# Weight halves 64 bytes into wider tiles, in a decoder trunk on one core

## The chip, the core and the metric

One of the eight cores of a Trainium2 chip runs the kernel. The metric is the device time of one execution in microseconds, taken as the median of several runs. A profile of one further execution of the kernel before is at hand, with its own time.

## The reference

The reference is a decoder trunk of two layers on 256 positions of width 2048, all in float32. Cut to what matters here:

```python
for layer in range(DEPTH):                                # 2
    shift, scale, gate = _adaln(c, ada_w[layer], ada_b[layer])
    h = x * (1.0 + scale) + shift
    if layer < N_A_LAYERS:                                # layer 0
        y = _ssd_mixer(h, a_in_w[i], ..., a_out_w[i])     # 2048 -> 10304, conv, scan, gate, 4096 -> 2048
    else:                                                 # layer 1
        y = _dilated_mixer(h, k_sh, v_sh, b_in_w[i], b_out_w[i])
    x = _layer_norm(ALPHA * x + (1.0 + gate) * y, ln_g[layer], ln_b[layer])
    if layer == N_A_LAYERS - 1:
        k_sh, v_sh = _shared_kv(x, kv_w)                  # 2048 -> 6144
```

Inside the mixer of layer 0, each of 8 groups forms scores from its B and C heads, masks them causally, and weights them by decays:

```python
cb = jnp.einsum("blgn,bsgn->blsg", cc, bc)
y_diag = jnp.einsum("blsgk,bsgkp->blgkp", cb[..., None] * decay, xc)
```

Most of the arithmetic lies in the big products of activations and weights (in_w, out_w, kv_w and the like).

## The kernel before

Weights stream in as pieces of 128 partitions by 1024 columns of float32 (`load_piece`, the tile `raw`, six buffers). `split` makes two halves of each piece in a rounded float32 type (`fp32r`): ScalarE copies the piece to `whi` (line 99), VectorE subtracts to get the remainder `wlo` (line 101), four buffers each. The activations are split in the same way and stay in SBUF in the tile `actT` (a high and a low half for each of 16 slices of the width). A product of two split factors is three matmuls: high by high, high by low, and low by high.

There are three forms of product, by what is loaded into TensorE as weights and what streams past it:

- `cm_piece` (channel-major, lines 150 to 152): slices of `whi` or `wlo` of 128 columns are loaded, 256 columns of `actT` stream by. It serves B, C and part of the inner x of layer 0; the small `dt` product (lines 612 to 614) has the same form.
- `cm_wide` (channel-major, lines 181 and 184): `whi` is loaded once for both halves of the activations, 512 columns (line 181); `wlo` for the high half alone, 256 columns (line 184). Two column blocks take turns, so four matmuls make a round. It serves the rest of the inner x, the keys, and the queries and gate of layer 1.
- `tm_mults` (token-major, lines 212 to 214): slices of `actT` (or of the scan's output) are loaded, 512 columns of `whi` or `wlo` stream by. It serves the z gate, the values and both output products.

`first_or` and `begin_next` start the first piece of the next product while the last piece of the current one is multiplied; `upcoming` is the list of those first pieces. In the first stage a list written out by hand (`order`) interleaves pieces of ten products with the dot products of the modulation (line 295), whose loads compete with the pieces.

For each group of the scan `stage1` makes a tile of three score blocks in PSUM (lines 716 and 717), multiplies it with a constant mask `cbmask` into `cb` (line 719: two triangles and a block of ones), builds the decays `seg` (line 732), and transposes the inner x (line 740) into PSUM tiles of the same pool of two. A scheduler places the instructions of the scan among the matmuls of the products.

Two tiles named `pad`, of 128 and 256 bytes per partition, are allocated and never used. A tile `ones` of 512 bytes stays in SBUF throughout; it serves the matmuls that warm TensorE up (line 435) and one sum (line 698). The pieces, halves and `actT` follow one another in SBUF behind the constants; as the program is built, each of them starts at a multiple of 256 bytes.

The lines that place the halves and the mask:

```python
hi, lo = into or [wp.tile([P, 1024], F32R, name=n, bufs=4) for n in ("whi", "wlo")]
copied.append(S.activation(hi, raw, AF.Copy))
latest.append(V.tensor_tensor(lo, raw, hi.bitcast(F32), op=ALU.subtract))
```

Of the kernel before, what the change touches and what calls it, by code (L numbers as in the profile page):

```python
# [18 lines left out]
P = 128  # L19
# [8 lines left out]
NG = 3  # L28
# [12 lines left out]
    _o += _s  # L41
NPAR = _o

CI, CT, CM, NCONST = 0, 128, 256, 640

CD, CG, NBIAS = 0, 384, 384 + 384 + 256

# [2 lines left out]
def trunk(ctx, tc, xT, x, c, par, cst, bias, lnrow, ada, wdt, win, wxs, wout, wk, wv, wbin, wbout, out):  # L50
# [20 lines left out]
    nc.scalar.dma_start(crow, c)  # L71
    cc = cons.tile([P, NCONST], F32, name="cc")

    cons.tile([P, 32], F32, name="pad")

    def pv(name):
        a, b = OFF[name]
        return prm[:, a - NB:b - NB]

    ident = cc[:, CI:CI + 128]  # L80
    tri = cc[:, CT:CT + 128]
    cbmask = cc[:, CM:CM + 384]
    ones = cons.tile([P, P], F32, name="ones")
    V.memset(ones, 1.0)


    def rows(t, b):

# [2 lines left out]
    def load_piece(src):  # L91
        raw = wp.tile([P, 1024], F32, name="raw", bufs=6)
        nc.sync.dma_start(raw, src)
        return raw

    def split(raw, into=None, after=None):

        hi, lo = into or [wp.tile([P, 1024], F32R, name=n, bufs=4) for n in ("whi", "wlo")]
        copied.append(S.activation(hi, raw, AF.Copy))  # L99
        with tc.issue_after(after) if after is not None else ExitStack():  # L100
            latest.append(V.tensor_tensor(lo, raw, hi.bitcast(F32), op=ALU.subtract))  # L101
        return hi.rearrange("p (k n) -> p k n", k=2), lo.rearrange("p (k n) -> p k n", k=2)
# [7 lines left out]
            with tc.issue_after(copied[-1].ins), tc.issue_after(latest[-1].ins):  # L110
                owed.pop(0)()

    def first_or(src, q):

        return ready.pop() if ready else split(load_piece(src[q]))

    def begin_next():

        if upcoming:
            src, q = upcoming.pop(0)  # L120
            ready.append(split(load_piece(src[q])))

    def behind_next():

# [15 lines left out]
    def cm_piece(src, q, ps, ahi, alo, k0=0, k1=KT, w=None, after=None, ks=(0, 1)):  # L140


        hi, lo = w or split(load_piece(src[q]), after=after)
        for k in ks:
            kt = 2 * q + k
            for n in range(4):
                o = ps[n // 2][:, n % 2, :]
                c_ = slice(n * P, n * P + P)
                first = kt == k0 and n % 2 == 0
                T.matmul(o, hi[:, k, c_], ahi[:, kt, :], start=first, stop=False, skip_group_check=True)  # L150
                T.matmul(o, hi[:, k, c_], alo[:, kt, :], start=False, stop=False, skip_group_check=True)  # L151
                T.matmul(o, lo[:, k, c_], ahi[:, kt, :], start=False, stop=kt == k1 - 1, skip_group_check=True)  # L152
# [4 lines left out]
    def cm_quad(src, ahi, alo, rate=(0, 1), k0=0):  # L157
        ps = acc_pair()
        for q in range(k0 // 2, KT // 2):
            w = first_or(src, q)  # L160
            if q == KT // 2 - 1:
                begin_next()
            cm_piece(src, q, ps, ahi, alo, k0=k0, w=w)
            background(*rate)
        return ps

    def cm_wide(src, dst, rate=(0, 1), moving=None, later=False):

        both, high = moving or (lambda kt: xp[:, kt], lambda kt: xhi[:, kt, :])
        ps = acc_pair()  # L170
        for q in range(KT // 4):
            w = first_or(src, q)
            if q == 1:
                settle()
            if q == KT // 4 - 1:
                begin_next()
            hi, lo = (t.rearrange("p k n -> p (k n)").rearrange("p (k n) -> p k n", k=4) for t in w)
            for k in range(4):
                kt = 4 * q + k
                for n in range(2):  # L180
                    T.matmul(ps[n], hi[:, k, n * P:n * P + P], both(kt), start=kt == 0, stop=False,  # L181
                             skip_group_check=True)
                for n in range(2):
                    T.matmul(ps[n][:, 0, :], lo[:, k, n * P:n * P + P], high(kt), start=False, stop=kt == KT - 1,  # L184
                             skip_group_check=True)
            background(*rate)
        def put():
            for n in range(2):
                S.activation(dst[:, n, :], ps[n][:, 1, :], AF.Copy)
                V.tensor_tensor(dst[:, n, :], ps[n][:, 0, :], dst[:, n, :], op=ALU.add)  # L190

        if later:
            owed.append(put)
        else:
            with behind_next():
                put()
# [45 lines left out]
        return V.tensor_tensor(dst_lo, val, dst_hi.bitcast(F32), op=ALU.subtract)  # L242


    sm.tile([P, 64], F32, name="pad", bufs=1)
    magic = cons.tile([P, 2], I32, name="magic")
    V.memset(magic, 0x5F3759DF)

# [85 lines left out]
    with ExitStack() as cA:  # L334
# [15 lines left out]
        with ExitStack() as cS:  # L350
# [78 lines left out]
            with ExitStack() as c0:  # L429
                pe = c0.enter_context(tc.tile_pool(name="pe", bufs=2))  # L430

                def warm(n, at, after=None):
                    for _ in range(n):
                        with tc.issue_after(after.ins) if after is not None else ExitStack():
                            after = T.matmul(at[:, 0, :P], ones, ones, start=True, stop=True)
                    return after

                at = mm.tile([P, 2, L], F32, name="acc")
# [70 lines left out]
                order = []  # L509
# [40 lines left out]

                def high_half(i):

                    halves[i] = [wp.tile([P, 1024], F32R, name=n, bufs=4) for n in ("whi", "wlo")]
                    copied.append(S.activation(halves[i][0][:, 512:], pieces[i][:, 512:], AF.Copy))

                def low_half(i):
# [47 lines left out]
                def dt_piece(q, raw):  # L604

                    if q == 0:
                        pss["dt"] = mm.tile([P, 2, L], F32, name="acc")[:, 0, :]
                    pd = pss["dt"]
                    hi, lo = (t.rearrange("p k n -> p (k n)").rearrange("p (k n) -> p k n", n=P) for t in split(raw))
# [12 lines left out]
                    V.tensor_copy(vv, pt)  # L622
# [11 lines left out]
                for i, (k, q, ends) in enumerate(order):  # L634
# [7 lines left out]
                    for j in (i, i + 1):  # L642
                        if j < len(order) and j not in halves and order[j][0] != "dt":
                            with tc.issue_after(highs[j // 2 - 1]) if j in (7, 9) else ExitStack():
                                halves[j] = split(pieces[j], after=dots[0] if j == 5 else None)
                    while ended:
                        put_away(*ended.pop())
                    if k == "dt":
# [61 lines left out]
            def stage1(g):  # L710
# [5 lines left out]
                T.matmul(pcb[:, 0:3:2, :], bm[:, 0:P], cm_, start=True, stop=True)  # L716
                T.matmul(pcb[:, 1, :], bm[:, P:L], cm_[:, P:L], start=True, stop=True)
                cb = px.tile([P, 3, P], F32, name="cb")
                V.tensor_tensor(cb, pcb, cbmask.rearrange("p (a n) -> p a n", a=3), op=ALU.mult)
                segs = []  # L720
                for w in range(2):
                    h0 = g * HPG + 4 * w
# [60 lines left out]

            def firsts(kind, g):
                if kind == "xs" and g > 1:
                    return [(wxs[2 * g - 4 + w], 0) for w in range(2)]
# [3 lines left out]
                return [(src, k0 // 2)]  # L790

            for g in range(G - 1):
                for kind in ("bc",) * (g % 2) + ("xs", "z"):
# [179 lines left out]
    with ExitStack() as cL:  # L973
# [47 lines left out]
        with tc.issue_after(tile4.ins):  # L1021
            state[0] = 0
            queue(pl, cols1[11:])
            jobs.append(lambda: gate_out(1))
            upcoming.extend((wk[2 * (2 * g + hq) + w], 0) for hq in range(2) for g in range(NG) for w in range(2))
            upcoming.extend((wv[1 + 2 * g], 0) for g in range(NG))
            evict_v(0, 2, tm_chunk(wv[4], hx, lx, rate=R))
            for hq in range(2):
                for g in range(NG):
# [43 lines left out]

    def queries(hq):
        qq = [pc2.tile([P, 4, L], F32, name=f"q{g}") for g in range(NG)]
        upcoming.extend([(wbin[2 * (2 * g + hq) + w], 0) for g in range(NG) for w in range(2)][1:])
# [225 lines left out]
def _layout(x, c, ada_w, ada_b, ln_g, ln_b, a_in_w, a_conv_w, a_conv_b, a_dt_bias,  # L1302
# [21 lines left out]
    cst[:, CI:CI + 128] = np.eye(P)  # L1324
    up = (i[:, None] <= i[None, :]).astype(f)
    cst[:, CT:CT + 128] = up
    cst[:, CM:CM + 384] = np.concatenate([up, up, np.ones((P, P), f)], 1)
    bias = np.zeros((P, NBIAS), f)
    same = 2 * (i[:, None] - i[None, :])
    near = np.concatenate([same + 1, same, same - 1], 1)  # L1330
# [42 lines left out]
```

## Time and profile before

| | |
|---|---|
| Median of 3 runs | 1238.09 us (1237.92 to 1238.58) |
| The profiled execution | 1238.06 us |
| Its span, first to last instruction | 1236.3 us |
| TensorE busy, matmuls | 99% of the span |
| VectorE, ScalarE busy | 83% and 57% |
| DMA queue of the big loads | 333.46 MB |

The span leaves out 1.8 us of the profiled execution, before the first instruction and after the last. PE is TensorE's matmuls, PEld its weight loads, which overlap them; DVE is VectorE, ACT is ScalarE, SP the engine that issues most DMAs. A group of instructions is told by line, engine, operation and tiles (written, then read), with the number of them, the time in which at least one ran, the mean length of one, and the idle time of the engine ahead of them. A matmul's length includes its way through the array, which overlaps the next matmul, so the lengths of a row of matmuls add up to more than the time they take.

### The profile page before, as it was taken

What the parts mean: (1) busy time and instruction counts of PE and PEld (TensorE: products, weight loads), DVE (VectorE), ACT (ScalarE), POOL (GpSimd) and SP (SyncE); (2) the same over time, 40 slices, a digit from 0 to 9 for tenths busy, and PEclk for the clock granted to TensorE, in tenths of its full rate; (3) what the DMA queues carried; (4) which work ended last, traced back from release to release, by engine and by line L of the source; (5) the groups of instructions that cost most, each with busy time, mean ns of one, the idle gap of its engine ahead of it and who ended that gap; (6) DMA issues with size and microseconds to landing.
All of it is one profiled execution on the core that took longest, in us unless ns stands there. A gap on an engine that the chain in (4) does not pass through costs nothing.

```text
span 1236.3 us, 18840 instructions
## 1 busy us (share of the span) xinstructions
PE 1224.5 (99%) x7132; PEld 1052.1 (85%) x7132; DVE 1027.6 (83%) x1456; ACT 702.8 (57%) x1050; POOL 3.9 (0%) x8
## 2 busy tenths in 40 slices
PE   8999999999999999999999999999999999999998
PEld 7889998898888888888888788888888888888886
DVE  6899986999988989899768678888978866758776
ACT  4555477868597789754335544434445644444551
POOL 0000000000000000000000000000000000000001
PEclk9999999999999999999999999999999999999999
DMA  9999977687666456699988569989997774464673
GB/s 378 423 421 422 421 252 248 230 291 253 215 197 206 169 166 210 205 337 351 365 315 296 194 201 359 363 339 370 381 396 291 230 257 145 122 192 133 205 256 68
DMA packets 81371, 336.05 MB, mean 272 GB/s; under 512 B 9200, under 2 KB 9856, under 8 KB 68480
## 3 DMA queue, kind: packets, MB, share of 16 engines
q1 hardware_dynamic: 80352, 333.46, 74.7%
q0 software_dynamic: 576, 1.05, 0.6%
q8 instruction: 56, 0.92, 0.3%
q10 hardware_dynamic: 352, 0.34, 0.1%
q14 instruction: 35, 0.29, 0.1%
HBM read 331.58 MB, written 3.23 MB: 271 GB/s over the span
## 4 chain that ended last, share of the span: by engine, by line
PE 91%; DMA 4%; DVE 2%; ACT 2%; issue 1%; SPq 0%; ACTq 0%; DVEq 0%
PE acc L181 24%; PE acc L213 13%; PE acc L214 13%; PE acc L212 13%; PE acc L184 12%; DMA raw<-in_win 3%; PE acc L150 3%; PE acc L152 3%; PE acc L151 3%; PE py L771 1%; DVE wlo L101 1%; ACT whi L99 1%; PE acc L981 1%; DMA adab<-in_par 1%; PE po L1112 1%
## 5 line engine op out<-in xcount | busy, mean ns | idle before, releaser
L99 ACT ACTIVATE whi<-raw 128x1024 fp32r<-128x1024 f32 x389 | 408.2, 1058 | 352.6 <-PE acc L214 132.8
L101 DVE TENSOR_TENSOR wlo<-raw,whi 128x1024 fp32r<-128x1024 f32 x389 | 468.9, 1221 | 145.0 <-ACT whi L99 139.0
L181 PE MATMUL acc<-actT,whi 128*128 128x512 f32 x1280 | 405.5, 397 | 0.0
L184 PEld LDWEIGHTS acc<-actT,wlo 128*128 128x128 f32 x1280 | 239.4, 188 | 55.6 <-DVE wlo L101 0.4
L213 PE MATMUL acc<-wlo,actT 128*128 128x512 f32 x656 | 257.3, 392 | 2.0 <-DVE wlo L101 2.0
L212 PE MATMUL acc<-whi,actT 128*128 128x512 f32 x656 | 253.4, 394 | 0.0
L184 PE MATMUL acc<-actT,wlo 128*128 128x256 f32 x1280 | 252.8, 279 | 0.0
L295 DVE SCALAR_TENSOR_TENSOR araw<-araw,cb__72 128x2048 f32<-128x2048 f32 x95 | 217.0, 2284 | 3.7 <-DMA araw<-in_ada 3.5
L181 PEld LDWEIGHTS acc<-actT,whi 128*128 128x128 f32 x1280 | 196.0, 189 | 0.4
L214 PE MATMUL acc<-whi,actT 128*128 128x512 f32 x432 | 169.0, 391 | 0.0
L213 PEld LDWEIGHTS acc<-wlo,actT 128*128 128x128 f32 x656 | 123.2, 188 | 29.0 <-DVE wlo L101 3.9
L212 PEld LDWEIGHTS acc<-whi,actT 128*128 128x128 f32 x656 | 122.7, 188 | 24.6 <-ACT s L632 0.5
L150 PE MATMUL acc<-actT,whi 128*128 128x256 f32 x372 | 104.3, 284 | 1.7 <-ACT actT L499 1.0
L151 PE MATMUL acc<-actT,whi 128*128 128x256 f32 x372 | 104.3, 283 | 0.0
L152 PE MATMUL acc<-actT,wlo 128*128 128x256 f32 x372 | 102.9, 284 | 0.8 <-DVE wlo L101 0.8
L214 PEld LDWEIGHTS acc<-whi,actT 128*128 128x128 f32 x432 | 81.1, 188 | 16.6
L214 PE MATMUL acc<-whi,ylo 128*128 128x512 f32 x224 | 87.5, 391 | 0.0
L150 PEld LDWEIGHTS acc<-actT,whi 128*128 128x128 f32 x372 | 71.0, 192 | 3.0 <-ACT actT L499 1.4
L151 PEld LDWEIGHTS acc<-actT,whi 128*128 128x128 f32 x372 | 71.3, 192 | 0.2
L152 PEld LDWEIGHTS acc<-actT,wlo 128*128 128x128 f32 x372 | 70.1, 192 | 1.4 <-DVE wlo L101 1.4
L214 PEld LDWEIGHTS acc<-whi,ylo 128*128 128x128 f32 x224 | 42.1, 188 | 8.5
L729 ACT ACTIVATE seg<-cbc,cumT 128x128 f32<-128x128 f32 x128 | 41.0, 389 | 5.1 <-DVE wlo L101 2.3
(310 smaller groups left out, 1153.6 us busy)
## 6 DMA issues: line engine op xcount, KB each, us to landing
araw<-in_ada SPq DMA_DIRECT2D x96, 1024.0 KB, 6.9
raw<-in_win SPq DMA_DIRECT2D x109, 512.0 KB, 6.0
raw<-in_wout SPq DMA_DIRECT2D x64, 512.0 KB, 5.5
raw<-in_wbin SPq DMA_DIRECT2D x64, 512.0 KB, 3.8
raw<-in_wxs SPq DMA_DIRECT2D x48, 512.0 KB, 4.5
raw<-in_wv SPq DMA_DIRECT2D x48, 512.0 KB, 6.3
raw<-in_wk SPq DMA_DIRECT2D x48, 512.0 KB, 7.4
cbc<-cumd SPq DMA_DIRECT2D x16, 512.0 KB, 4.9
```

The source lines that it names most:

```text
L99: copied.append(S.activation(hi, raw, AF.Copy))
L101: latest.append(V.tensor_tensor(lo, raw, hi.bitcast(F32), op=ALU.subtract))
L150: T.matmul(o, hi[:, k, c_], ahi[:, kt, :], start=first, stop=False, skip_group_check=True)
L151: T.matmul(o, hi[:, k, c_], alo[:, kt, :], start=False, stop=False, skip_group_check=True)
L152: T.matmul(o, lo[:, k, c_], ahi[:, kt, :], start=False, stop=kt == k1 - 1, skip_group_check=True)
L181: T.matmul(ps[n], hi[:, k, n * P:n * P + P], both(kt), start=kt == 0, stop=False, skip_group_check=True)
L184: T.matmul(ps[n][:, 0, :], lo[:, k, n * P:n * P + P], high(kt), start=False, stop=kt == KT - 1, skip_group_check=True)
L212: T.matmul(o, h_, hi[:, k, :], start=kt == k0, stop=False, skip_group_check=part)
L213: T.matmul(o, h_, lo[:, k, :], start=False, stop=False, skip_group_check=part)
L214: end = T.matmul(o, l_, hi[:, k, :], start=False, stop=kt == k1 - 1, skip_group_check=part)
L295: return V.scalar_tensor_tensor(raw, raw, 1.0, cb_, op0=ALU.mult, op1=ALU.mult, accum_out=mod[layer][:, ct, j:j + 1])
L729: S.activation(seg[:, hh, b, :], cbc[:, hh, b, :], AF.Relu, bias=cumT[:, b, h0 + hh:h0 + hh + 1], scale=-1.0)
```

## The change

The halves `whi` and `wlo` get tiles of 1088 columns (4352 bytes), of which 1024 are used. Each user says how many columns into the tile its halves begin: `SHORT`, 16 columns or 64 bytes, for the channel-major products (`cm_piece`, `cm_wide`, the `dt` product and the two hand-made halves of the first pieces), `LONG`, none, for the token-major ones. The list `upcoming` carries the offset along. To make room, the constants shrink: `cbmask` goes, `ones` becomes a part of the loaded constants, the pads go, and the warm-up has a tile of ones of its own in a pool that ends with the first stage. The masking of the scores becomes two operations: a multiplication of two blocks with the triangle, and a copy of the third.

```diff
-CI, CT, CM, NCONST = 0, 128, 256, 640
+CI, CT, CM, NCONST = 0, 128, 256, 384
...
-    cons.tile([P, 32], F32, name="pad")
-
...
-    cbmask = cc[:, CM:CM + 384]
-    ones = cons.tile([P, P], F32, name="ones")
-    V.memset(ones, 1.0)
-
+    ones = cc[:, CM:CM + 128]
+    SHORT, LONG = (16, 16), (0, 0)
...
-    def split(raw, into=None, after=None):
-
-        hi, lo = into or [wp.tile([P, 1024], F32R, name=n, bufs=4) for n in ("whi", "wlo")]
+    def halves_at(off):
+
+        return [wp.tile([P, 1088], F32R, name=n, bufs=4)[:, o:o + 1024] for n, o in zip(("whi", "wlo"), off)]
+
+    def split(raw, into=None, after=None, off=(0, 0)):
+
+        hi, lo = into or halves_at(off)
...
-        hi, lo = w or split(load_piece(src[q]), after=after)
+        hi, lo = w or split(load_piece(src[q]), after=after, off=SHORT)
...
-            w = first_or(src, q)
+            w = first_or(src, q, SHORT)
...
-    sm.tile([P, 64], F32, name="pad", bufs=1)
...
+                full = pe.tile([P, P], F32, name="ones", bufs=1)
+                V.memset(full, 1.0)
+
...
-                            after = T.matmul(at[:, 0, :P], ones, ones, start=True, stop=True)
+                            after = T.matmul(at[:, 0, :P], full, full, start=True, stop=True)
...
-                V.tensor_tensor(cb, pcb, cbmask.rearrange("p (a n) -> p a n", a=3), op=ALU.mult)
+                V.tensor_tensor(cb[:, 0:2, :], pcb[:, 0:2, :], tri[:, None, :].to_broadcast([P, 2, P]), op=ALU.mult)
+                V.tensor_copy(cb[:, 2, :], pcb[:, 2, :])
...
-            upcoming.extend((wk[2 * (2 * g + hq) + w], 0) for hq in range(2) for g in range(NG) for w in range(2))
-            upcoming.extend((wv[1 + 2 * g], 0) for g in range(NG))
+            upcoming.extend((wk[2 * (2 * g + hq) + w], 0, SHORT) for hq in range(2) for g in range(NG) for w in range(2))
+            upcoming.extend((wv[1 + 2 * g], 0, LONG) for g in range(NG))
...
-    cst[:, CM:CM + 384] = np.concatenate([up, up, np.ones((P, P), f)], 1)
+    cst[:, CM:CM + 128] = 1.0
```

The constants ahead of the pieces lose 1024 + 128 + 512 = 1664 bytes, the eight tiles of halves gain 256 each, and a pad of 256 goes behind them. So pieces, halves and `actT` now start 128 bytes past a multiple of 256, the channel-major halves 64 further on, and what lies behind moves up by 128 bytes.

The matmuls of the products stand in the same order throughout. In the scan the two-step mask moves what stands around it. On VectorE at the first scores (`cb` is the masked tile, `aux` the PSUM tile of scores, `cacc` the convolution of the next group's inner x), before:

```order
L719 TENSOR_TENSOR cb<-aux,cc 128x384
L368 SCALAR_TENSOR_TENSOR cacc<-s_97,prm,cacc 128x255 x2
L368 SCALAR_TENSOR_TENSOR cacc<-s_97,prm,cacc 128x254 x2
L368 SCALAR_TENSOR_TENSOR cacc<-s_97,prm,cacc 128x253 x2
L368 SCALAR_TENSOR_TENSOR cacc<-s_97,prm,cacc 128x255
L732 TENSOR_TENSOR seg<-seg,cb 128x1024
L368 SCALAR_TENSOR_TENSOR cacc<-s_97,prm,cacc 128x254
```

and with the change:

```order
L722 TENSOR_TENSOR cb<-aux,cc 128x256
L367 SCALAR_TENSOR_TENSOR cacc<-s_93,prm,cacc 128x255 x2
L367 SCALAR_TENSOR_TENSOR cacc<-s_93,prm,cacc 128x254 x2
L367 SCALAR_TENSOR_TENSOR cacc<-s_93,prm,cacc 128x253 x2
L367 SCALAR_TENSOR_TENSOR cacc<-s_93,prm,cacc 128x255
L723 COPY cb<-aux 128x128
L367 SCALAR_TENSOR_TENSOR cacc<-s_93,prm,cacc 128x254
L736 TENSOR_TENSOR seg<-seg,cb 128x1024
```

The multiplication keeps its place; the copy comes seven convolution steps later, and the PSUM tile is free only then. On TensorE, in the z product beside these scores, the four transposes of the inner x (`aux<-cc,xs`) stand before:

```order
L212 MATMUL acc<-whi,actT 128x512
L213 MATMUL acc<-wlo,actT 128x512
L740 MATMUL aux<-cc,xs 128x128 x4
L214 MATMUL acc<-whi,actT 128x512
L212 MATMUL acc<-whi,actT 128x512
```

and with the change, 13 matmuls further on in the same product:

```order
L213 MATMUL acc<-wlo,actT 128x512
L214 MATMUL acc<-whi,actT 128x512
L744 MATMUL aux<-cc,xs 128x128 x4
L212 MATMUL acc<-whi,actT 128x512
L213 MATMUL acc<-wlo,actT 128x512
```

In later groups transposes, score products and conversions of pieces change places in the same way, by a few instructions.

More of the change, by code (lines that the diff above doesn't have):

```diff
@@ L111, in settle, with first_or @@
                 owed.pop(0)()
-    def first_or(src, q):
-        return ready.pop() if ready else split(load_piece(src[q]))
+    def first_or(src, q, off=(0, 0)):
+        return ready.pop() if ready else split(load_piece(src[q]), off=off)
     def begin_next():
         if upcoming:
-            src, q = upcoming.pop(0)
-            ready.append(split(load_piece(src[q])))
+            src, q, off = upcoming.pop(0)
+            ready.append(split(load_piece(src[q]), off=off))
     def behind_next():
@@ L171, in cm_wide @@
         for q in range(KT // 4):
-            w = first_or(src, q)
+            w = first_or(src, q, SHORT)
             if q == 1:
@@ L551, in high_half @@
                 def high_half(i):
-                    halves[i] = [wp.tile([P, 1024], F32R, name=n, bufs=4) for n in ("whi", "wlo")]
+                    halves[i] = halves_at(SHORT)
                     copied.append(S.activation(halves[i][0][:, 512:], pieces[i][:, 512:], AF.Copy))
@@ L608, in dt_piece @@
                     pd = pss["dt"]
-                    hi, lo = (t.rearrange("p k n -> p (k n)").rearrange("p (k n) -> p k n", n=P) for t in split(raw))
+                    hi, lo = (t.rearrange("p k n -> p (k n)").rearrange("p (k n) -> p k n", n=P) for t in split(raw, off=SHORT))
                     for k in range(8):
@@ L644, in trunk @@
                             with tc.issue_after(highs[j // 2 - 1]) if j in (7, 9) else ExitStack():
-                                halves[j] = split(pieces[j], after=dots[0] if j == 5 else None)
+                                halves[j] = split(pieces[j], after=dots[0] if j == 5 else None,
+                                                  off=LONG if str(order[j][0])[0] == "z" else SHORT)
                     while ended:
@@ L785, in firsts @@
                 if kind == "xs" and g > 1:
-                    return [(wxs[2 * g - 4 + w], 0) for w in range(2)]
+                    return [(wxs[2 * g - 4 + w], 0, SHORT) for w in range(2)]
                 src, k0, _ = begun.get((kind, g), (None, 0, None))
@@ L789, in firsts @@
                     src = win[{"bc": g // 2, "xs": 4 + g, "z": 6 + g}[kind]]
-                return [(src, k0 // 2)]
+                return [(src, k0 // 2, LONG if kind == "z" else SHORT)]
             for g in range(G - 1):
@@ L1075, in queries @@
         qq = [pc2.tile([P, 4, L], F32, name=f"q{g}") for g in range(NG)]
-        upcoming.extend([(wbin[2 * (2 * g + hq) + w], 0) for g in range(NG) for w in range(2)][1:])
+        upcoming.extend([(wbin[2 * (2 * g + hq) + w], 0, SHORT) for g in range(NG) for w in range(2)][1:])
         for g in range(NG):
```

## The prediction

> **What bounds the kernel now.** I read the page's engine shares first, then the chain that ended last, then stretches of the program.
>
> ```profile
> span 1236.3 us, 18840 instructions
> PE 1224.5 (99%) x7132; PEld 1052.1 (85%) x7132; DVE 1027.6 (83%) x1456; ACT 702.8 (57%) x1050; POOL 3.9 (0%) x8
> PE 91%; DMA 4%; DVE 2%; ACT 2%; issue 1%; SPq 0%; ACTq 0%; DVEq 0%
> PE acc L181 24%; PE acc L213 13%; PE acc L214 13%; PE acc L212 13%; PE acc L184 12%; DMA raw<-in_win 3%; PE acc L150 3%; PE acc L152 3%; PE acc L151 3%; PE py L771 1%; DVE wlo L101 1%; ACT whi L99 1%; PE acc L981 1%; DMA adab<-in_par 1%; PE po L1112 1%
> ```
>
> TensorE is busy for 99% of the span and carries 91% of the chain: the kernel is a row of matmuls with hardly a hole. So what counts is the time from the start of one matmul to the start of the next, and what a neighbour costs only where it holds TensorE up. The longest wait of TensorE on another engine's tile and the stretches say how much room the others have.
>
> ```profile
> PE acc L213 <- DVE wlo L101: 2.0, 4, 0.8
> core 0: us, PE busy (x) PEld busy (x) DVE busy (x) ACT busy (x) POOL busy (x), PEclk, DMA share, GB/s
> 0.00:130.00 130.00, 123.98 (x762) 111.95 (x763) 112.89 (x129) 67.57 (x92) 0.20 (x4) 1.00 1.01 411
> 250.00:520.00 270.00, 270.00 (x1841) 230.05 (x1841) 247.53 (x427) 212.31 (x366) 0.00 (x0) 1.00 0.64 210
> 775.00:960.00 185.00, 184.68 (x984) 157.94 (x983) 157.65 (x169) 83.29 (x110) 0.00 (x0) 1.00 0.92 353
> ```
>
> In the first 130 us the DMA engines are full (1.01), so faster matmuls gain nothing there. In the scan (250 to 520) VectorE has 247.5 of 270 us, 92%; in the keys (775 to 960) it has 85% and DMA 0.92. The clock granted is 1.00 throughout.
>
> The groups of matmuls that the change touches, and three stretches in which nearly one kind runs alone (channel-major pieces of 256 columns, token-major pieces, wide channel-major pieces), for the pace:
>
> ```profile
> L181 PE MATMUL acc<-actT,whi 128*128 128x512 f32 x1280 | 405.5, 397 | 0.0
> L184 PE MATMUL acc<-actT,wlo 128*128 128x256 f32 x1280 | 252.8, 279 | 0.0
> L150 PE MATMUL acc<-actT,whi 128*128 128x256 f32 x372 | 104.3, 284 | 1.7 <-ACT actT L499 1.0 <-ACT s L632 0.7
> 0.00:130.00 130.00, 43.00 (x156) 29.50 (x156) 1.00 1.01 411
> 110.00:140.00 30.00, 30.00 (x251) 1.00 1.02 421
> 590.00:660.00 70.00, 70.00 (x310) 1.00 0.86 315
> 780.00:880.00 100.00, 100.00 (x576) 1.00 0.93 361
> ```
>
> The first stretch row is that of line 150 alone. A matmul's 397 or 284 ns is a length that overlaps the next; the pace comes from counts. With one or two matmuls at the edges counted twice: 30/250 = 120 ns for 256 columns (line 150 and its two followers), 70/309 = 226.5 ns for the token-major 512, and 100/574 x 4 = 697 ns for a four of the wide product (two of line 181 with 512 columns, two of line 184 with 256). The timeline splits such a four:
>
> ```profile
> 785.33 0.63 PE L181 MATMUL acc<-actT,whi 128*128 128x512 f32 x2
> 785.80 0.39 PE L184 MATMUL acc<-actT,wlo 128*128 128x256 f32 x2
> 785.92 0.30 PEld L181 LDWEIGHTS acc<-actT,whi 128*128 128x128 f32 x2
> 786.03 0.63 PE L181 MATMUL acc<-actT,whi 128*128 128x512 f32 x2
> 786.26 0.42 PEld L184 LDWEIGHTS acc<-actT,wlo 128*128 128x128 f32 x2
> 786.49 0.40 PE L184 MATMUL acc<-actT,wlo 128*128 128x256 f32 x2
> ```
>
> Line 181 takes 0.47 us for two (235 each), then 0.46 (230); line 184 takes 0.23 for two, 115 each. So equal shapes go at different paces: 256 columns at 115 or 120, 512 at 226.5 or 230 to 235, with the weight load beside each. Something between the streaming of one matmul and the load for the next costs several ns, and it isn't fixed.
>
> **The change part by part.** *The offset.* Nothing is added to or taken from the matmuls; 64 bytes are put between where the weights of channel-major products lie (whi and wlo as the loaded side) and where the activations lie. In the program as built, whi, wlo and actT all start at multiples of 256 bytes before. After, actT and the token-major halves start 128 past such a multiple and the channel-major halves 192 past. So every distance between two streams that the trace holds is a multiple of 256 bytes in these products; no row has 64, and the price must be bounded from both sides.
>
> The lower end: the least that a matmul with its own weight load costs here is that of the float32 products of the scores.
>
> ```profile
> 308.63 0.59 PE L716 MATMUL aux<-bcm 128*128 128x256 f32 x2
> 309.06 0.38 PE L717 MATMUL aux<-bcm 128*128 128x128 f32 x2
> ```
>
> Two passes start 0.43 us apart in all, 215 ns each for 256 columns. If a float32 column costs two of the others, which the trace doesn't show directly, 512 columns in the other products could go at 215 and 256 at 107.5: a four at 645 instead of 697, and 120 to 107.5 for line 150's kind. There are 1280/2 = 640 fours: 640 x 52 = 33.3 us. Of 3 x 372 = 1116 short matmuls 3 x 156 = 468 lie in the DMA-bound start; 648 x 12.5 = 8.1 us. That end is -41.4 us.
>
> The Trainium skill ("TensorE: Matmul & The Clock Gate", Back-to-back issue gap) has N/2.4 + 2.5 ns between isolated matmuls, so 215.8 and 109.2. The trace's 226.5 and 120 stand 11 above it and decide; an estimate by that page's figures would put a four at 650 and this end near -37 us.
>
> The upper end: a stretch just after the switch from channel-major to token-major, in which the two streams aren't yet in step.
>
> ```profile
> 150.51 0.63 PE L212 MATMUL acc<-whi,actT 128*128 128x512 f32 x2
> 150.97 0.39 PE L213 MATMUL acc<-wlo,actT 128*128 128x512 f32 x1
> ```
>
> Two of line 212 take 0.46 us, 230 to 233 each against 226.5 settled: up to 6.5 ns more for the same work. Wide fours at the slow rows (235 and 120) are 710: 640 x 13 = +8.3 us; the short ones 6.5 slower, 1116 x 6.5 = +7.3 us (a slower matmul counts in the first 130 us too, TensorE being busy for 124 of them). That end is +15.6 us.
>
> I take the value between: the channel-major matmuls fall to the best pace their shapes show already, 226.5 for 512 columns and 115 for 256. A four is then 683: 640 x 14 = -9.0 us; the short ones, 648 x 5 = -3.2 us. It is a choice: the rows show that an equal shape can run that fast here, not that 64 bytes bring it. Were it so, VectorE in the scan would have some 248.7 of 267 us, 93%, and DMA in the keys 0.93: both still early enough.
>
> *The mask in two steps.* One VectorE operation per group becomes two.
>
> ```profile
> L719 DVE TENSOR_TENSOR cb<-aux,cc x8: 548/550/558, 219.5 to 495.1; 128x384 f32<-128x384 f32 x8
> L190 DVE TENSOR_TENSOR xs<-acc,xs x24: 410/417/425, 271.3 to 487.0; 128x256 f32<-128x256 f32 x24
> L699 DVE COPY cumT<-aux x1: 284/284/284, 196.2 to 196.2; 128x128 f32<-128x128 f32 x1
>   PEld aux L740: 1.7, 5
> ```
>
> 417 + 284 - 550 = 151 ns, 8 times: 1.2 us of VectorE, with over 20 us idle in that stretch. What feels it is the transposes of line 740, which wait for the score tile to be read (1.7 us of weight loads, 5 times); the last row is from the list of who waits for the mask. 5 x 151 ns = +0.8 us if nothing hides it, 0 if all is hidden; I take 0.8. The order shows that the copy also stands further down: at the first scores it comes behind seven convolution steps, and the transposes go 13 places later on TensorE, where a matmul of a product takes their place. That can turn either way, by about the waits that stand there now (2 us), so it widens the range by 1 us.
>
> *Ones, the short constants, the pads.* The fill of the warm-up's ones is the same instruction in another pool and one place later on VectorE, at a time when TensorE would wait as much as now: 0. The constants' load shrinks from 640 to 384 columns, 0. Dropped pads cost no instruction; they only move addresses.
>
> Sum: -9.0 - 3.2 + 0.8 = -11.4 us. The profiled execution took 1238.06 us for a span of 1236.3, and the median of the runs is 1238.09, so the sum is made against either: 1226.7 us.
>
> **The rivals.** *Nothing but the reorder (0.20).* The 12 ns between 226.5 and 215 may be a cost of each matmul that no address changes. For it: the settled pace, 226.5 and 120, is the same through long stretches whatever slice is read, at many distances that are multiples of 256. Against it: 115 beside 120. Time: 1238.06 + 0.8 = 1238.9, from 1237 to 1241.
>
> The Trainium skill ("SBUF — State Buffer", Who interferes with whom) gives TensorE two read ports, one for the moving side and one for weight loads, and has it wait on no one. By that rule this rival is the outcome; the trace's 115 and 120 for one shape don't contradict it outright but leave room for more.
>
> *The other side (0.34).* The 64 bytes put the load out of the step into which it settles now. Then lines 181, 184 and 150 to 152 keep the pace that they show only after a switch. It decides from the point where a four takes over 697 + 2.5/0.64 = 701 ns. At the full end, 1238.06 + 15.6 + 0.8 = 1254.5; with about half of it, which I hold likelier, 1246. For it: the present steady state is better than its starting phase. Against: a wide four isn't at the best of its rows now.
>
> *All of it (0.10).* The excess disappears: -41.4 + 0.8, so 1197.5. Against it: no product of this kind comes near 215 in a settled stretch.
>
> **How the numbers follow.** The forecast, a partial gain, has 0.36 and by itself runs from 1219 to 1234 (half to nearly twice the gain on fours and short ones, and 1 us for the reorder). About 0.2%, 2.5 us, is what a measurement of this kernel can tell from no change. Faster: 0.36 + 0.10 = 0.46. Of the 0.20 for the reorder alone 0.15 lies within 0.2% and 0.05 above; so same 0.15, slower 0.34 + 0.05 = 0.39. The range leaves out the case of all the gain (0.10) and the upper part of the other side (0.09): 1212 to 1249.
>
> **What would show it.** Right: in the wide stretch a four under 690 ns (over 580 matmuls in 100 us), in the short stretch under 118 ns each, token-major still at 226.5. The mask as 417 and 284 ns, and line 740's successor waiting no more than 3 us. Wrong: the same counts as now (the reorder alone), fewer than 570 in 100 us of the wide product (the other side), or VectorE or DMA waits ahead of matmuls that eat what the pace gives. A token-major pace that moves would mean that the start of the tiles itself counts, which I give nothing.

## The result, and the profile after

The kernel after took 1235.65 us (median of 15 runs, 1234.91 to 1236.85), the kernel before 1238.44 us beside it (15 runs); ratio 0.998, 95% interval 0.9972 to 0.9988. It is faster by 2.8 us, where 11.4 were forecast. The profiled execution has a span of 1234.5 us, 1.8 us less. It took 1236.29 us, 0.6 above the median, and the profiled one before took 1238.06, 0.4 below its median of 15: the two traces hold 1.8 of the 2.8 us, and the other 1.0 is this choice of executions.

Engine shares, loads by slice and the chain of the kernel after, from its page; the row of loads of the kernel before stands ahead of it, and the first five slices are 0 to 154 us:

```profile
GB/s 378 423 421 422 421 252 248 230 291 253 215 197 206 169 166 210 205 337 351 365 315 296 194 201 359 363 339 370 381 396 291 230 257 145 122 192 133 205 256 68
```

```profile
span 1234.5 us, 18854 instructions
PE 1220.3 (99%) x7132; PEld 1049.4 (85%) x7132; DVE 1028.0 (83%) x1464; ACT 701.6 (57%) x1048; POOL 3.9 (0%) x8
GB/s 373 414 414 415 413 283 244 216 305 247 222 204 205 171 172 205 203 337 353 365 316 294 195 204 362 356 341 371 378 382 313 224 261 147 122 201 124 207 256 69
PE 84%; DMA 6%; DVE 6%; ACT 2%; issue 1%; ACTq 0%; DVEq 0%
```

TensorE is as full as before, with 4.2 us less busy time in a span that is 1.8 us shorter. In the first slices the loads come at 414 instead of 422 GB/s. The stretches of the prediction, kernel after (TensorE busy, matmuls, clock, DMA share, GB/s):

```profile
0.00:130.00 130.00, 122.86 (x754) 0.99 1.00 404
110.00:140.00 30.00, 30.00 (x249) 1.00 1.02 414
590.00:660.00 70.00, 70.00 (x310) 1.00 0.87 313
780.00:880.00 100.00, 100.00 (x579) 1.00 0.93 361
```

Token-major is where it was (310). The wide stretch goes from 576 to 579 matmuls. The stretch of short products has 249 instead of 251, though its products follow one another faster: it stands in the part that waits for loads. The timeline of the kernel after shows the fours of the wide product:

```profile
784.77 0.62 PE L181 MATMUL acc<-actT,whi 128*128 128x512 f32 x2
785.23 0.39 PE L184 MATMUL acc<-actT,wlo 128*128 128x256 f32 x2
785.47 0.62 PE L181 MATMUL acc<-actT,whi 128*128 128x512 f32 x2
785.93 0.40 PE L184 MATMUL acc<-actT,wlo 128*128 128x256 f32 x2
786.16 0.62 PE L181 MATMUL acc<-actT,whi 128*128 128x512 f32 x2
786.62 0.39 PE L184 MATMUL acc<-actT,wlo 128*128 128x256 f32 x2
786.85 0.39 PE L181 MATMUL acc<-actT,whi 128*128 128x512 f32 x1
```

From 784.77 to 786.85 are three fours, 693 ns each. A pace below is worked out from the records as the mean time from one matmul's start to the next one's, over settled stretches. By that a four fell from 696.8 to 693.8 ns (line 181: 233.1 to 230.9 each; line 184: 115.3 to 116.0). A short product of lines 150 to 152 went from 120.0 to one of two settled paces, 113.3 or 117.8, each of which holds for dozens of products (mean 116.2). The dt product went from 120 to 113.

The waits of TensorE, kernel after:

```profile
PE acc L150 <- ACT s L634: 2.0, 1, 2.0
PE acc L213 <- DVE wlo L101: 1.9, 4, 0.8
PE acc L152 <- DVE wlo L101: 1.6, 3, 0.6
PE cps L450 <- DVE crow L444: 1.2, 1, 1.2
PE acc L437 <- DVE ones L432: 1.1, 1, 1.1
PE acc L150 <- ACT actT L501: 0.9, 1, 0.9
PE aux L744 <- DVE cb L723: 0.7, 1, 0.7
```

The first wait, of 2.0 us, ends at 32 us, and the granted clock around it is below 1:

```profile
31.00:45.00 14.00, 12.75 (x97) 0.88 1.02 413
```

A mean of 0.88 over 14 us is what about 3.4 us at half the clock give; behind the wait the products of 256 columns start 213 ns apart for that long, and 113 ns after it. The kernel before has 1.00 there.

Comparing the start of the same matmul (the k-th on TensorE) in the two traces gives the balance by time. At 145 us the kernel after is 1.3 us behind; at 250 us, 0.9; from there it gains 2.7 us and ends 1.8 ahead. It gains where channel-major products run, and nothing between 520 and 780 us, where nearly all are token-major. The late gain adds up: 640 fours x 3.0 ns = 1.9 us, and the short products after 250 us, 160 to 170 of them at 116 instead of 121 ns, 0.8 us. The two questions for the experiments are why the four fell so little, and what costs time in the first 145 us.

### The profile page after: what moved, and what is told of

It is laid out like the page before. It is cut to its first block, busy times and chain, and to the rows that moved or that the text cites. A ratio compares the mean times of both kernels' runs of the same rounds, so it can differ in the third digit from the quotient of the medians.

```text
span 1234.5 us, 18854 instructions
## 1 busy us (share of the span) xinstructions
PE 1220.3 (99%) x7132; PEld 1049.4 (85%) x7132; DVE 1028.0 (83%) x1464; ACT 701.6 (57%) x1048; POOL 3.9 (0%) x8
## 4 chain that ended last, share of the span: by engine, by line
PE 84%; DMA 6%; DVE 6%; ACT 2%; issue 1%; ACTq 0%; DVEq 0%
PE acc L181 24%; PE acc L184 12%; PE acc L213 12%; PE acc L214 12%; PE acc L212 12%; DMA raw<-in_win 5%; DVE araw L294 3%; DVE wlo L101 2%; PE py L775 1%; PE acc L150 1%; PE acc L152 1%; PE acc L151 1%; DMA araw<-in_ada 1%; ACT whi L99 1%; PE acc L985 1%
```

## The experiments

Two theories on the pace. A: it depends on how far apart, in bytes, the two things that TensorE reads lie, the loaded block and the streamed rows. B: addresses don't matter. On the start there are again two. D: the 128 bytes by which all pieces and halves moved slow their loads. M: the two-step mask and the new order cost it.

**pace: the products alone, at 15 placements.** The trunk is left out; token-major, short and wide products run one after the other on loaded halves that begin so many columns (4 bytes each) into their tiles:

```diff
+    for name, s, t in PLACES:
+        hi, lo = whi[:, s:s + 1024], wlo[:, t:t + 1024]
```

> The kernel leaves the whole trunk out and only multiplies: for 15 placements of the high and low halves (columns of 4 bytes between the start of the weights and a multiple of 1024 bytes at which the activations start: 0, 4, 8, 12, 16, 20, 24, 28, 32, 48 for both; then (0,16), (16,0), (16,32), (16,48) for (high, low); then 0 again) it runs, twice each, a token-major, a short and a wide channel-major product, with no other engine at work. Theory A (the distance between loaded weights and streamed columns sets the step into which the two settle): short matmuls at 120 ns for 0 and near 113 or 118 for 16; a wide four at 697 for 0 and 694 for 16; other distances give other paces, each constant within a product or switching once. Rival B (the pace does not hang on the distance; the absolute start or the traffic of the other engines made the difference): all placements give the same pace, within 1 ns, for each form.

Three groups of the trace by mean length, at 0, at 16 columns, and with the high half at 16 and the low one at 48:

```profile
L78 PE MATMUL short_a<-act,whi 128*128 128x256 f32 x128 | 23.1, 283 | 0.0
L78 PE MATMUL short_e<-act,whi 128*128 128x256 f32 x128 | 22.3, 279 | 0.0
L78 PE MATMUL short_n<-act,whi 128*128 128x256 f32 x128 | 22.0, 277 | 0.0
```

Start to start these are 120.0 ns at 0; 117.8 in one pass and 113.3 in the other at 16 columns; 113.3 in both at (16, 48). At 28 columns it is 120 again. Token-major is best at 0 (226.7) and 229 to 233 elsewhere, so leaving those products at 0 was right. B falls.

**pace2: all pairs.** The trunk is left out; the two halves each at 0, 16, 32 or 48 columns, with the activations laid out as the kernel's.

> Again the trunk is left out and only products run, now with the activations laid out as in the trunk (high and low halves apart for the mixer, side by side for keys and queries) and all 16 pairs of 0, 16, 32, 48 columns for the high and the low half. Theory A: each pair has its own pace in each of the three forms; (0, 0) short at 120 and the wide fours near 697, (16, 16) short at 113 or 118 and fours near 694, and (16, 48) short at 113 only. If a pair is better than (16, 16) in all forms it goes into the trunk. Rival B: within 1 ns of each other.

Settled pace in ns, short product / wide four, worked out from the starts (rows: the high half's columns, across: the low half's):

```
        0            16           32           48
 0   120.0/696.5  117.8/700    119/700      117.8/693.1
16   117.8/713.0  117.8/693.4  118.2/700.5  113.3/693.1
32   118.2/706.6  118.8/704.6  120/698      116.7/705.2
48   117.7/700    113.3/703.5  115.6/702.5  117.8/689.8
```

The kernel before and the kernel after are on this table: 696.5 for the 696.8 in its trace, 693.4 for 693.8. So the offset of 16 columns is worth 3 ns a four, and no pair is worth 14. Some pairs are 16 ns worse than none.

**short0: the kernel after with its channel-major halves at 0.**

```diff
-    SHORT, LONG = (16, 16), (0, 0)
+    SHORT, LONG = (0, 0), (0, 0)
```

> The changed kernel with all halves at column 0 of their wider tiles: only the 64 bytes are undone; tiles of 4352 bytes, shifted starts, two-step mask and the other order stay. Theory A (the 64 bytes made the gain): short matmuls back at 120 ns, a wide four at 697, and the time back to that of before or up to 1 us above it, so 1238.1 to 1239.5 us. Rival B (the starts, the tiles' stride or the other order made it): short matmuls at 113 to 118 still, time 1235.6 us.

1240.09 us, ratio 1.0015 (1.0006 to 1.0024). The paces are back at 120.0 and 697, so the wider tiles as such do nothing to them. The 64 bytes are worth 0.35% (1.0015 to 0.998), some 4 us by these ratios, and the rest of the change costs 1.9 us; it is this rest that puts the time 0.6 us above the range expected.

**mask: the kernel before with the mask in two steps.**

```diff
-                V.tensor_tensor(cb, pcb, cbmask.rearrange("p (a n) -> p a n", a=3), op=ALU.mult)
+                V.tensor_tensor(cb[:, 0:2, :], pcb[:, 0:2, :], tri[:, None, :].to_broadcast([P, 2, P]), op=ALU.mult)
+                V.tensor_copy(cb[:, 2, :], pcb[:, 2, :])
```

> The kernel before with the mask in two steps and nothing else. If the two steps cost what was forecast: 417 + 284 ns on VectorE in place of 550, 0 to 0.8 us more in all, so 1238.1 to 1239.3 us. Rival: the reordering that comes with it gives time back, down to the changed kernel's 1235.6 us.

1238.03 us beside 1237.96, ratio 1.0001 (0.9992 to 1.001). The wait for the masked scores grows from 0.5 to 1.3 us in the profile,

```profile
PE aux L741 <- DVE cb L720: 1.3, 1, 1.3
```

and the median doesn't show it. The profiled execution does: it took 1239.8 us, the longest of the 11, and falls 0.8 us behind the profile before between 204 and 229 us, where this wait lies. By the medians M isn't what costs the 1.9 us.

**nopad and pad: the 128 bytes by themselves.** The first takes the unused tile of 128 bytes out of the constants of the kernel before; the second puts it back into the kernel after.

```diff
-    cons.tile([P, 32], F32, name="pad")
```

> The kernel before without its pad of 128 bytes, nothing else: all starts behind the constants move by 128 bytes. Theory D: 414 GB/s in the first 130 us and 1240 us. Rival E: 422 GB/s and 1238 us.

> The changed kernel with a pad of 128 bytes put back among the constants, so that pieces and activations start at multiples of 256 bytes again (channel-major halves 64 behind one). Theory D (the shift of all starts by 128 bytes slows the loads of the DMA-bound start, 414 GB/s against 422, and takes back some 2 us of what the 64 bytes give): loads at 421 to 423 GB/s in the first 130 us, time near 1235.6 - 2 = 1233.7 us. Rival E (the loads are slower through another order of transfers, and the shift does nothing): 414 GB/s and 1235.6 us.

nopad took 1240.75 us, ratio 1.0017 (1.0008 to 1.0026), and pad 1234.31 us, ratio 0.9969 (0.9957 to 0.998). Loads by slice, nopad and then pad:

```profile
GB/s 374 413 414 415 413 281 244 223 302 244 219 202 204 170 158 217 195 339 350 364 318 294 196 204 357 357 338 371 378 400 294 230 254 147 122 196 128 207 255 68
```

```profile
GB/s 377 423 420 422 421 254 243 223 301 248 219 203 207 170 171 205 211 338 348 364 313 301 190 204 349 370 342 371 379 396 298 230 256 145 122 201 125 206 257 69
```

D holds both ways: with tiles 128 bytes past a multiple of 256 the loads run at 414 GB/s, with tiles on the multiple at 422. Over the four full slices (123 us) 2% is 2.3 us, and nopad loses 2.1 (1238.4 x 0.0017). The intervals of pad and of the kernel after overlap, so pad's 1.4 us would not do alone; the starts of the matmuls bear it out. At 145 us the profiles with shifted tiles (after, nopad, short0, high16) are 1.3 to 2.0 us behind the profile before, those without (pad, mask and the four variants of best further down) between 0.2 behind and 1.3 ahead. The stretch at half the clock has no part in it: best has one at the same place and is 0.1 behind at 145 us. Which of the moved tiles does it (the pieces that the DMAs write are the likeliest) wasn't tried.

The Trainium skill ("DMA: Bandwidth & Descriptors", How a descriptor splits into AXI transactions) has transfers split at multiples of 256 bytes, where a start off the multiple pays for the bytes before it. An estimate by that page for 4096 bytes from 128 past a multiple is 132 units of 32 bytes instead of 128 units, 3% more; the trace's 2% agrees in sign and about in size, though the page speaks of bytes that are fetched, and what is off here is a tile that is written.

**high16: the pair (16, 0).** In the expectation, and in those of best, "weights" stands for the high half and "streamed side" for the low one: both are loaded sides, and the pair means the same as in pace2. Nor do the wide products of high16 stay as they were: `cm_wide` takes its offsets from `SHORT` too, so their low half goes back to 0 as well.

```diff
-    SHORT, LONG = (16, 16), (0, 0)
+    SHORT, LONG = (16, 0), (0, 0)
```

> The kernel after with the weights 16 columns in and the streamed side at 0 for the short pieces (the wide ones as in the kernel after). Theory A with the bench's paces: short products 117.8 ns instead of 113.3 to 117.7 (up to +1 us), and where a wide four then falls in the same layout as on the bench, 713 ns instead of 694 (640 x 19 = +12.5 us): 1236 to 1248 us, the wide four's own pace telling which. Rival (any shift between the two sides is worth the same): within 1 us of 1235.6.

1248.96 us, ratio 1.0076 (1.0061 to 1.0092), 1 us past the slow end expected. The timeline of high16:

```profile
784.93 0.64 PE L181 MATMUL acc<-actT,whi 128*128 128x512 f32 x2
785.41 0.41 PE L184 MATMUL acc<-actT,wlo 128*128 128x256 f32 x2
785.65 0.64 PE L181 MATMUL acc<-actT,whi 128*128 128x512 f32 x2
786.12 0.41 PE L184 MATMUL acc<-actT,wlo 128*128 128x256 f32 x2
786.36 0.63 PE L181 MATMUL acc<-actT,whi 128*128 128x512 f32 x2
786.83 0.41 PE L184 MATMUL acc<-actT,wlo 128*128 128x256 f32 x2
787.08 0.64 PE L181 MATMUL acc<-actT,whi 128*128 128x512 f32 x2
```

Three fours in 2.15 us, 717 each here; the settled mean over the whole trace is 714. The bench had 713. So 640 fours x 20 ns = 12.8 us; the kernel lost 13.3 us against the kernel after by the medians, 11.9 by the ratios.

**pace3: what the excess is made of.** The trunk is left out. Besides the plain form: both sides moved by 16 columns (moved), the halves alone (apart), the loaded block one repeated column (oneweight), the streamed side one repeated column (onecolumn).

```diff
+    def one(t):
+        return t[:, 0:1].to_broadcast([P, P])
+    def streamed(t, fixed):
+        return t[:, 0:1].to_broadcast([P, t.shape[-1]]) if fixed else t
```

> The trunk is left out; only products run, token-major and short ones, in five forms: plain (distance 0), moved (both sides 16 columns in), apart (weights alone 16 columns in), oneweight (weights loaded from one repeated column), onecolumn (streamed side is one repeated column). Theory A (only the distance between the two sides counts): moved equals plain, 120 and 226.7 ns; apart 113 to 118 and about 229 ns. If the excess over the fastest pace comes from the two sides' reads meeting in memory, oneweight and onecolumn fall below plain. Rival (a fixed cost per product, whatever is read): oneweight and onecolumn stay at 120 and 226.7 ns.

Groups by mean length:

```profile
L75 PE MATMUL token_plain<-whi,act 128*128 128x512 f32 x96 | 31.0, 402 | 18.1 <-ACT whi L69 18.1
L75 PE MATMUL token_oneweight<-whi,act 128*128 128x512 f32 x96 | 30.1, 392 | 0.0
L75 PE MATMUL token_onecolumn<-whi,act 128*128 128x512 f32 x96 | 28.9, 380 | 0.0
L75 PE MATMUL short_plain<-act,whi 128*128 128x256 f32 x128 | 23.1, 283 | 0.0
L75 PE MATMUL short_moved<-act,whi 128*128 128x256 f32 x128 | 23.1, 283 | 0.0
L75 PE MATMUL short_apart<-act,whi 128*128 128x256 f32 x128 | 21.9, 276 | 0.0
L75 PE MATMUL short_oneweight<-act,whi 128*128 128x256 f32 x128 | 21.9, 276 | 0.0
L75 PE MATMUL short_onecolumn<-act,whi 128*128 128x256 f32 x128 | 21.5, 274 | 0.0
```

Start to start, short and token-major, in ns (settled part):

```
plain       120.0   226.7
moved       120.0   226.7
apart       113.3   228.8
oneweight   113.3   231.0
onecolumn   111.7   216.4
```

Moving both sides by 16 columns changes nothing, moving one does: the distance counts, not the place. (Nor does moving all tiles by 128 bytes: nopad's paces are 119.9 and 696.7.) A streamed side that is one column takes 10.3 ns of a token-major product away and 8.3 of a short one. So at least that much is not a fixed cost per product; it hangs on what is read as the streamed side. (One repeated column changes the values as well as the addresses; that the values matter was not ruled out.) One repeated loaded column gives 113.3 for a short product but 231.0 for a token-major one, so it isn't the load alone either. That the two reads meet in the same part of the memory would be compatible with these rows, but it is a guess: no view shows the meeting.

**best and best2: the best pairs and the pad.** The kernel pad, with (16, 48) for the short products and (48, 48) for the wide ones; best2 is the same kernel again.

```diff
-    SHORT, LONG = (16, 16), (0, 0)
+    SHORT, WIDE, LONG = (16, 48), (48, 48), (0, 0)
```

> The kernel after with its 128-byte pad back, the short pieces' weights 16 columns and their streamed side 48 columns in, the wide pieces 48 and 48. Theory A (the pace depends on how the two sides of a product lie to each other, and the bench's paces hold in the kernel): short products settle at 113.3 ns everywhere, a wide four at about 690 ns, so 640 x 3.7 = 2.4 us less on the wide side and up to 648 x 2.9 = 1.9 us less on the short one: 1230 to 1232 us. Rival (bench paces do not carry over to the kernel, where other engines read and write the same memory): 1234.3 us as with the pad alone, within 1 us.

> The kernel best once more, beside its two variants. Its profile waits 1.9 us at the transposes for the masked scores' copy, once, and falls 2.0 us behind the kernel pad between 204 and 229 us; the paces are those of the bench. If that wait belongs to the kernel, 1233 us again; if it belongs to one execution, the median can lie up to 1 us lower.

best took 1233.38 us, ratio 0.9956 (0.9943 to 0.9968), best2 1232.7 us, ratio 0.9954 (0.9941 to 0.9966). The times miss the 1230 to 1232 us expected; best lies within 1 us of the rival's 1234.3, best2 1.6 below it. It is the paces that decide against the rival, since they carried over: a four 690, short products 113.7 throughout. From 250 us on the profile of best gains 1.6 us over pad's, two thirds of the 2.4 expected of the fours. Before that it gains nothing and falls 2.0 us behind between 204 and 229 us, with this wait for the copy of the mask in the middle:

```profile
PE aux L745 <- DVE cb L724: 2.0, 2, 1.9
```

In the profile of best2 (span 1230.9 us, against 1233.9) the longest of these waits is 1.1 us and the loss is gone, so it belongs to single executions. Only part of it is the wait; the clock makes the rest. The ten microseconds around it, best and then best2 (the clock stands behind the bracket):

```profile
219.00:229.00 10.00, 8.12 (x31) 0.83 0.43 151
219.00:229.00 10.00, 8.88 (x66) 1.00 0.36 115
```

A mean of 0.83 is 3.4 of 10 us at half the clock, and for that long token-major products start 427 ns apart instead of 227. The stretches of best2:

```profile
110.00:140.00 30.00, 29.23 (x252) 1.00 1.02 422
780.00:880.00 100.00, 100.00 (x582) 1.00 0.95 365
```

With short products at 113.7 ns TensorE stands idle for 0.8 of these 30 us and does no more of them (252): the loads are the limit there. In the wide stretch 582 matmuls stand where 576 stood.

**bestact and bestswap: the mask again.** best with the third block copied by ScalarE, and best with the copy written ahead of the multiplication.

```diff
-                V.tensor_copy(cb[:, 2, :], pcb[:, 2, :])
+                S.activation(cb[:, 2, :], pcb[:, 2, :], AF.Copy)
```

> The kernel best, with the copy of the third score block on ScalarE instead of VectorE (the order gives it a place of its own there; VectorE loses eight copies of 0.28 us). If the copy's late place on VectorE costs the 1 to 2 us that best lost at its first scores, 1231.5 to 1232.5 us and no wait of the transposes over 0.7 us; if not, as best2 within 0.7 us.

> The kernel best, with the copy written ahead of the multiplication, so that from the second group on the two stand next to each other on VectorE. Same prices: 1231.5 to 1232.5 us if the distance between the two operations costs the 1 to 2 us, at the first scores it stays five places and the wait there stays too (then 1232.5 to 1233); as best2 if the mask is hidden anyway.

1233.05 us, ratio 0.9957 (0.9945 to 0.997), and 1232.78 us, ratio 0.9958 (0.9945 to 0.9972), beside 1232.7 for best2. Neither moves the median, though bestswap's profile has a wait of 2.5 us at the transposes:

```profile
PE aux L745 <- DVE cb L724: 2.6, 2, 2.5
```

That execution took 1235.15 us, 2.4 over its median: behind the wait the clock is halved again (0.83 from 219 to 229 us), and it falls 3.0 us behind best2's profile between 204 and 229. Bestact's longest wait is 1.2 us, over the 0.7 that its expectation set, and the clock stays at 1.00. So the two-step mask costs the medians nothing that these runs can tell, in either order, but 2 to 3 us in an execution in which its wait grows to 1.9 us or more.

## Why the prediction was right in direction and wrong in size

*The offset is a real mechanism, and its sign was right.* 64 bytes change the pace of the same matmuls at the same clock, token-major stays at 226.7, and the rival of the reorder alone (1237 to 1241) is refuted by short0 against the kernel after. The rule of the Trainium skill that stood beside that rival ("SBUF — State Buffer", Who interferes with whom) gives TensorE independent ports for its two reads; by pace and pace3 the pace depends on how the two lie to each other, so in time they are not independent here, and the measurement decides.

*The size of the four was the failing step.* "The channel-major matmuls fall to the best pace their shapes show already" took 226.5 for 512 columns from the token-major product, another form with its two sides at another distance. The four fell by 3.0 ns, not 14: 1.9 us instead of 9.0. A pace that a shape has at one distance doesn't carry over to another; with the sides exchanged, the same shift even makes token-major products slower. The prediction's own signs say the same: 579 matmuls in the wide stretch, not over 580, and a four not under 690 ns, while the short products (under 118) and token-major came out as it asked.

*The short products fell by 3.8 ns on the mean, near the 5 forecast, but the gain could only be had later.* The prediction ended the part that waits for loads at 130 us. The window after that shows that it goes on, in the kernel before too; behind it stands the next window of the kernel after:

```profile
130.00:155.00 25.00, 25.00 (x200) 1.00 1.02 421
155.00:205.00 50.00, 48.97 (x301) 1.00 0.72 245
```

DMA is at 1.02 until 155 us. From there to 205 us it is at 0.72, but TensorE's busy time falls to 48.97 us (49.55 before): the faster products only waited more, twice 0.5 us for `wlo` instead of once. The 309 short products between 130 and 205 us took 37.3 us before, 305 took 37.6 after (start to start, waits included). Only from 205 us on did they gain, 4 ns each on 350, 1.4 us instead of 3.2.

*"Dropped pads ... only move addresses"* was taken as nothing, and cost 1.4 us (pad against the kernel after) to 2.1 us (nopad). The move by 128 bytes stood in the description of the change, and the first 130 us were known to be bound by DMA; the two weren't put together.

*The mask:* 418 and 281 ns in the trace, for 417 and 284; the transposes wait 0.7 us for it (0.5 before). The term of +0.8 is 0 in the medians (mask, bestact, bestswap); that a longer wait costs clock as well stood in neither the sum nor the range.

With the measured sizes the sum is -1.9 - 1.4 + 1.4 to 2.1, so -1.2 to -1.9 us (the paces give the offset 3.3 us, where the ratios of short0 gave it some 4). The profiles, from which the sizes come, differ by 1.8. The medians differ by 1.0 more, since the two profiled executions lie on opposite sides of theirs; why executions differ by that much stays open.

*The other side* has a real mechanism, given 0.34: high16 shows it, with fours at 714 ns, a little over the 710 of that end, and short products that gained (118.0). Which side a shift falls on is not told by its size, since (16, 16) and (16, 0) differ by one half's 64 bytes. The 235 ns came from the timeline of a wide four, not from the switch, which gave 230 to 233; to the nanosecond that line's steps are 231 to 236, 233.1 on the mean. As a bound it was nearly right: line 181 settles at 235.2 in high16. *All of it* (0.10) has no placement among those tried: the best of 16 pairs are 113.3 and 689.8, and only a streamed side of one column comes near the bound, at 111.7 and 216.4.

## What to carry to other kernels

Where TensorE is full and each matmul loads its own weights, as here, the distance in bytes between the loaded block and the streamed rows sets the pace: 113.3 to 120.0 ns for 256 columns, 6%. It can't be reasoned out from one shape's pace at another distance, but a bench of bare products over a few offsets of both halves gave the wide fours of four kernels within about 1 ns, two of them before they ran. When tiles are moved by some bytes, look at what the DMAs write as well: 128 bytes past a multiple of 256 took 2% from loads that were at their limit, and a third to a half of what the offset had brought. A profile is of one execution: look at its clock and at its place among the runs before a microsecond of it is put down to the change.

## What was not expected of the hardware

Waits of TensorE of 1.88 and 2.17 us (best), 1.95 (after) and 2.49 (bestswap) were each followed by about 3.4 us at half the granted clock; waits of up to 1.86 us (mask, at 32 us) were not. Ahead of 145 us, where the loads were the limit, the loss was made up again; at 224 us it stayed.

One program can settle at two paces at the same placement: at (16, 16) short products ran at 113.3 or 117.8 ns. Within its rows of them the kernel after changes over at 137, 146 and 161 us, each time where TensorE was held up for a moment; why, was not tried. At (16, 0) the two passes of pace gave 117.8 and 122.3, while at (16, 48) both passes of pace and pace2 gave 113.3. Ten of the 16 short paces of pace2 are 113.3, 117.8 or 120.0 to 0.1 ns, the others lie between. The excess over the pace with one streamed column (216.4 ns for 512 columns, 111.7 for 256) was between 1.6 and 8.3 ns for the short products over the pairs of pace2.
